# Token block sums in two column halves, and another product order in the first weight pair, in an encoder block in float32

## The chip, the cores and the metric

The kernel runs on one core of one Trainium2 chip. The metric is the device time of one execution in microseconds; the median of three runs of the kernel before is 762.26 us (760.61 to 762.30). The engines are called by name: TensorE (PE in the rows) multiplies, VectorE (DVE) adds and subtracts, ScalarE (ACT) copies, rounds and applies functions, GpSimd (POOL) does small odd jobs and issues some DMAs, and SyncE (SP) issues the loads.

## What is computed

A transformer encoder block on 512 tokens of 1024 channels: two attention branches merged by gates, then a feed-forward stage. Only the last matters here.

```python
x = x + rmsnorm(merged @ w_out[l], post_mix_w[l])
h = rmsnorm(x, pre_ffn_w[l])
f = (jax.nn.silu(h @ w_gate[l]) * (h @ w_up[l])) @ w_down[l]
x = x + rmsnorm(f, post_ffn_w[l])
```

`w_gate` and `w_up` are 1024 x 2816. Everything is float32.

## The kernel before

**Precision.** TensorE takes operands rounded to float32r. So each operand is split into a high part (a rounded copy, made by ScalarE) and a low part (the rest, made by a subtraction on VectorE), and each product is three matmuls: high x high, high x low, low x high (`mm3`, L205 to L208, or L1016 to L1018).

**The tokens.** After the attention stage the loop at L918 takes four token tiles of 128. For each it multiplies by `w_out` and norms twice: `scaled` (L892) squares and scales the product, `post` (L903) adds it to x, sums the squares (`add_square`, L888), lets GpSimd make the reciprocal root (`rms_r`, L307), and scales the result to `h2` (L913). `to_Q` (L856) transposes `h2` on TensorE (L864), and writes the high part (L866), the low part (L867) and a float32 copy (L868, `HR`). The tokens are held as four blocks B11, B12, B21, B22: the first index is the half of the 1024 channels, the second the half of the 512 tokens. Token tiles 0 and 1 make the columns of B11 and B21, tiles 2 and 3 those of B12 and B22, 128 columns each.

**The feed-forward stage.** The first 256 columns of `w_gate` and of `w_up` (`UF`, four weight units) are multiplied in the plain way, first with the first half of the tokens and then with the second (loop at L976). Tile 3 is transposed in the middle of the last unit of the first half (L985), and the token sums follow (`t_sums`, L872). The other columns come as 20 pairs of weight tiles, gate and up in turn (loop at L1005). Each pair is a 2 x 2 block product made in seven products of blocks instead of eight, by the Strassen-Winograd scheme: the weight blocks A11 to A22 are combined to S1 to S4, the token blocks to T1 to T4. A product is 12 matmuls of 128 x 256 columns (four steps of 128 channels, three matmuls each), so a pair is 84. The token sums are made once for all pairs:

```python
for nm, a, b in (("T1", b12, b11), ("T2", b22, "T1"), ("T3", b22, b12), ("T4", b21, "T2")):
    t[nm] = U(F32, [128, 4, 256], "Tr")
    nc.vector.tensor_sub(t[nm], a, t[b] if isinstance(b, str) else b)
```

with a high part `Th` (L880) and a low part `Tl` (L881) of each.

**The weights of a pair** are prepared in six steps (`pair_steps`, L63), one behind each product of the pair ahead; for the first pair they are spread over the second half of the loop at L976 (L992, L993). Step `s0` splits A11 and A12 together: ScalarE makes the high part (L70) and a negated copy of it (L72), and GpSimd issues a DMA that adds the raw weights to the negated copy, which gives the low part (L73). `s1` adds S2 and S1 on VectorE (L94, L95), `s2` splits them (L70, and L75 on VectorE), `s3` and `s4` do the same for S3 and S4 (L105, L106), and `s5` splits A22, by DMA again. The parts of S3 and S4 are kept in the place of the second half's upper token block `Q[0, 1]`, which the pairs don't read.

**Order.** Up to the end of the value projections the order is written by hand. From there on a scheduler orders each engine's queue by its own estimate of times, keeping the dependencies; so the written order of the stages here is only its input. Each engine works through its queue in order. Eight PSUM banks (`psB`) go round among the transposes, the first feed-forward columns and the pairs.

Of the kernel before, what the change touches and what calls it, by code (L numbers as in the profile page):

```python
# [8 lines left out]
F32 = mybir.dt.float32  # L9
F32R = mybir.dt.float32r  # L10
AF = mybir.ActivationFunctionType
# [4 lines left out]
D = 1024  # L16
# [16 lines left out]
def dram(ap, offset, pattern):  # L33
    return bass.AP(tensor=ap.tensor, offset=ap.offset + offset, ap=pattern)
# [136 lines left out]
def block_kernel(ctx: ExitStack, tc: tile.TileContext, x, pre_mix_w, w_in,  # L171
# [3 lines left out]
    nc = tc.nc  # L175
# [22 lines left out]
    def U(dt, shape, name, pool=None):  # L198
        return (pool or up).tile(shape, dt, tag="u", name=name)
# [5 lines left out]
    def mm3(bank, sh, sl, mh, ml, first, last):  # L205
        nc.tensor.matmul(bank, sh, mh, start=first, stop=False)  # L206
        nc.tensor.matmul(bank, sh, ml, start=False, stop=False)  # L207
        nc.tensor.matmul(bank, sl, mh, start=False, stop=last)  # L208
# [15 lines left out]
    for nm, c0 in (("vb", 2560), ("va", 1024)):  # L224
        for j in range(4):
            n = w_in.shape[1]
            src = dram(w_in, c0 + 2 * j * 128 * n,
                       [[n, 128], [128 * n, 2], [1, 512]])
# [131 lines left out]
    v = {}  # L360
# [441 lines left out]
    psB = pstk.enter_context(tc.tile_pool(name="psB", bufs=6, space=PSUM))  # L802
# [11 lines left out]
    for m in range(8):  # L814
        bank = pmm.tile([128, 512], F32, tag="mm", name="mm")
# [4 lines left out]
        hi, lo = W.get(UG["a", m])  # L820
# [4 lines left out]
        hi, lo = W.get(UBR["a", m // 2])  # L825
        cs = slice(128 * (m % 2), 128 * (m % 2) + 128)
# [4 lines left out]
        t = U(F32R, [128, 2, 512], "mg")  # L831
# [6 lines left out]
    psB = ctx.enter_context(tc.tile_pool(name="psC", bufs=8, space=PSUM))  # L838
# [6 lines left out]
    for b in range(NB):  # L845
        t = U(F32, [128, D], "x2")
# [7 lines left out]
    HR = {}  # L854

    def to_Q(h, b):  # L856
        n, cs = b // 2, slice(128 * (b % 2), 128 * (b % 2) + 128)
        for g in range(2):
            if (g, n) not in HR:
                HR[g, n] = U(F32, [128, 4, 256], "HR")  # L860
            tb = psB.tile([128, 4, 128], F32, tag="b", name="tb")
            for k in range(4):
                kk = 4 * g + k
                nc.tensor.transpose(tb[:, k], h[:, 128 * kk:128 * kk + 128], ident)  # L864
            hi, lo, raw = Q[g, n][:, 0, :, cs], Q[g, n][:, 1, :, cs], HR[g, n][:, :, cs]
            nc.scalar.activation(hi, tb, AF.Copy)  # L866
            nc.vector.tensor_sub(lo, tb, hi.bitcast(F32))  # L867
            nc.scalar.activation(raw, tb, AF.Copy)  # L868

    TQ = {}  # L870

    def t_sums():  # L872

        b11, b12, b21, b22 = HR[0, 0], HR[0, 1], HR[1, 0], HR[1, 1]
        t = {}
        for nm, a, b in (("T1", b12, b11), ("T2", b22, "T1"), ("T3", b22, b12), ("T4", b21, "T2")):
            t[nm] = U(F32, [128, 4, 256], "Tr")
            nc.vector.tensor_sub(t[nm], a, t[b] if isinstance(b, str) else b)
            hi, lo = U(F32R, [128, 4, 256], "Th"), U(F32R, [128, 4, 256], "Tl")
            nc.scalar.activation(hi, t[nm], AF.Copy)  # L880
            nc.vector.tensor_sub(lo, t[nm], hi.bitcast(F32))  # L881
            TQ[nm] = hi, lo
        for nm, q in (("B11", Q[0, 0]), ("B21", Q[1, 0]), ("B22", Q[1, 1])):
            TQ[nm] = q[:, 0], q[:, 1]

# [32 lines left out]
    for b in range(NB):  # L918
# [6 lines left out]
        for n, k0, k1 in parts:  # L925
            if b and n == 1 and k0 == 4:
                to_Q(h2[b - 1], b - 1)
            for k in range(k0, k1):
                hi, lo = W.get(UO[k])
# [13 lines left out]
    F = []  # L943

    def ff_out(G, Uu):

        f = U(F32, [128, 2, 512], "f", up2 if len(F) < 11 else up)
        nc.scalar.activation(f, G, AF.Sigmoid)
        nc.vector.tensor_mul(f, f, G)
        nc.vector.tensor_mul(f, f, Uu)  # L950
        F.append(f)
# [13 lines left out]
    def steps_of(n):  # L965
        if n >= len(pairs):
            return []
        return W.pair_steps(pairs[n], lambda: U(F32, [128, 1024], "S"))
# [7 lines left out]
    for half in range(2):  # L976
        cs = slice(256 * half, 256 * half + 256)
        for m in range(2):
            for nm in ("g", "u"):
                last = half == 0 and m == 1 and nm == "u"  # L980
                bank = bb[nm, m][:, cs]
                hi, lo = W.get(UF[nm, m])
                for k in range(KD):
                    if last and k == 4:
                        to_Q(h2[3], 3)  # L985
                        t_sums()
                    q = Q[k // 4, half]
                    mm3(bank, hi[:, k], lo[:, k], q[:, 0, k % 4], q[:, 1, k % 4],
                        k == 0, k == KD - 1)
                if half == 1:  # L990
                    W.drop(UF[nm, m])
                    first = first or steps_of(0)  # L992
                    first.pop(0)()  # L993
    for fn in first:
        fn()
    G, Uu = U(F32, [128, 2, 512], "G"), U(F32, [128, 2, 512], "G")
    for m in range(2):
# [1 line left out]
        nc.vector.tensor_copy(Uu[:, m], bb["u", m])  # L999
    ff_out(G, Uu)  # L1000

    ORDER = (("A11", "B11", "A"), ("S2", "T2", "B"), ("S1", "T1", "C"), ("S3", "T3", "D"),
             ("S4", "B22", "C"), ("A12", "B21", "A"), ("A22", "T4", "D"))
    gu = {}
    for n, unit in enumerate(pairs):  # L1005
        nxt = steps_of(n + 1)
        parts = W.parts.pop(unit)
        bank = {c: psB.tile([128, 512], F32, tag="b", name="b")[:, :256] for c in "ABCD"}
        G = U(F32, [128, 2, 512], "G")
        pv = U(F32, [128, 3, 256], "pv")  # L1010
        for i, (sn, tn, c) in enumerate(ORDER):
            (sh, sl), (th, tl) = parts[sn], TQ[tn]
            for k in range(4):
                fst, lst = i < 4 and k == 0, k == 3
                kw = {"skip_group_check": True} if i >= 4 else {}
                nc.tensor.matmul(bank[c], sh[:, k], th[:, k], start=fst, stop=False, **kw)  # L1016
                nc.tensor.matmul(bank[c], sh[:, k], tl[:, k], start=False, stop=False, **kw)  # L1017
                nc.tensor.matmul(bank[c], sl[:, k], th[:, k], start=False, stop=lst, **kw)  # L1018
            B = bank[c]
            if i == 0:  # L1020
                nc.scalar.activation(pv[:, 0], B, AF.Copy)
            elif i == 1:
                nc.vector.tensor_add(pv[:, 1], pv[:, 0], B)
            elif i == 2:
                nc.vector.tensor_add(pv[:, 2], pv[:, 1], B)
            elif i == 3:
                nc.vector.tensor_add(G[:, 1, 256:], pv[:, 2], B)
            elif i == 4:
                nc.vector.tensor_add(G[:, 0, 256:], pv[:, 1], B)
            elif i == 5:  # L1030
                nc.scalar.activation(G[:, 0, :256], B, AF.Copy)
            else:
                nc.vector.tensor_add(G[:, 1, :256], pv[:, 1], B)
            if nxt:
                nxt.pop(0)()
        gu[n % 2] = G
        if n % 2:
            ff_out(gu[0], gu[1])
# [42 lines left out]
    for b in range(NB):  # L1081
        f_split()
        t = U(F32, [128, D], "x2")
        nc.sync.dma_start(t, x2d[b])
        x2.append(t)
    for b in range(NB):
# [6 lines left out]
        for n in range(2):  # L1093
            c = slice(512 * n, 512 * n + 512)
# [71 lines left out]
```

## Time and profile before

| | kernel before |
|---|---|
| median of 3 runs | 762.26 us (760.61 to 762.30) |
| the profiled execution | 761.96 us |
| its span in the profile | 760.0 us |
| TensorE busy | 738.8 us (97%) |
| VectorE busy | 481.5 us (63%) |
| ScalarE busy | 373.8 us (49%) |
| GpSimd busy | 85.1 us (11%) |
| mean of all DMA traffic | 134 GB/s |

Busy shares are over the whole span; the change concerns a stretch of some 30 us around 425 us, where the pairs begin. Times in the rows are microseconds from the start of the span. In a row of the timeline the first number is the start, the second the duration, and the bracket at its end tells how long the engine had been idle before and what it then waited for. `x2` is two instructions in one row.

### The profile page before, as it was taken

How to read it: one execution, taken by the hardware profiler on the slowest of the kernel's cores; microseconds unless marked ns; L12 is line 12 of the kernel's file. 1: busy time of each engine (PE TensorE's matmuls, PEld its weight loads, DVE VectorE, ACT ScalarE, POOL GpSimd, SP SyncE). 2: the span in 40 equal slices, each digit the busy share in tenths (PEclk: the TensorE clock that was granted, in tenths of full speed). 3: DMA queues.
4: the chain of work that ended last, by engine and by line, in shares of the span. 5: the costliest groups of instructions: out<-in, count | busy, mean ns of one | idle time of the engine just before them, and what ended most of it. 6: DMA issues, size and time to landing. Idle time of an engine off the chain costs nothing.

```text
span 760.0 us, 11245 instructions
## 1 busy us (share of the span) xinstructions
PE 738.8 (97%) x4360; PEld 650.6 (86%) x4360; DVE 481.5 (63%) x827; ACT 373.8 (49%) x604; POOL 85.1 (11%) x130
## 2 busy tenths in 40 slices
PE   7999999999999999999999799999999999999996
PEld 5887888877888888887889799999999998888884
DVE  5625688888776633564456787778877789232333
ACT  4414565665666732452224566666666667222211
POOL 2001011122330000000110111111111110000000
PEclk9999999999999999999999899999999999999998
DMA  9537646333311122464514487778788774453112
GB/s 257 171 98 201 159 124 160 98 97 97 97 56 57 56 83 84 131 201 131 147 55 139 97 164 180 182 177 196 174 193 194 183 197 149 138 167 109 58 41 70
DMA packets 102724, 102.01 MB, mean 134 GB/s; under 512 B 3552, under 2 KB 85488, under 8 KB 102672
## 3 DMA queue, kind: packets, MB, share of 16 engines
q1 hardware_dynamic: 96224, 83.34, 38.0%
q0 software_dynamic: 6448, 17.97, 12.2%
q8 instruction: 34, 0.56, 0.3%
q14 instruction: 18, 0.15, 0.1%
HBM read 75.08 MB, written 4.19 MB: 104 GB/s over the span
## 4 chain that ended last, share of the span: by engine, by line
PE 85%; DVE 6%; ACT 4%; DMA 2%; issue 1%; SPq 0%; POOL 0%; DVEq 0%; POOLq 0%; ACTq 0%
PE b L1016 9%; PE b L1018 9%; PE b L206 9%; PE b L1017 9%; PE b L208 9%; PE b L207 9%; PE mm L206 7%; PE mm L208 7%; PE mm L207 7%; PE mm L375 5%; DMA raw<-in_w_in_dram 2%; PE s L669 1%; DVE pl L620 1%; ACT p L586 1%; PE t L708 1%
## 5 line engine op out<-in xcount | busy, mean ns | idle before, releaser
L146 DVE TENSOR_TENSOR w<-raw,w 128x1024 fp32r<-128x1024 f32 x67 | 82.1, 1226 | 85.4 <-ACT w L140 84.9
L140 ACT ACTIVATE w<-raw 128x1024 fp32r<-128x1024 f32 x67 | 70.4, 1053 | 64.3 <-PE b L208 52.6
L206 PE MATMUL mm<-hT,w 128*128 128x512 f32 x256 | 101.3, 396 | 0.2 <-DVE v L387 0.2
L208 PE MATMUL mm<-hT,w 128*128 128x512 f32 x256 | 100.6, 393 | 0.0
L207 PE MATMUL mm<-hT,w 128*128 128x512 f32 x256 | 100.1, 391 | 0.0
L1016 PE MATMUL b<-Th,w 128*128 128x256 f32 x240 | 68.8, 287 | 4.5 <-ACT w L70 4.5
L1018 PE MATMUL b<-Th,w 128*128 128x256 f32 x240 | 68.8, 288 | 0.0
L1017 PE MATMUL b<-Tl,w 128*128 128x256 f32 x240 | 68.6, 286 | 0.0
L208 PEld LDWEIGHTS mm<-hT,w 128*128 128x128 f32 x256 | 48.1, 188 | 10.7
L206 PEld LDWEIGHTS mm<-hT,w 128*128 128x128 f32 x256 | 48.1, 188 | 10.3 <-DVE v L387 0.6
L207 PEld LDWEIGHTS mm<-hT,w 128*128 128x128 f32 x256 | 48.1, 188 | 9.9
L206 PE MATMUL b<-w,fh 128*128 128x512 f32 x144 | 56.1, 390 | 0.0
L208 PE MATMUL b<-w,fl 128*128 128x512 f32 x144 | 56.1, 390 | 0.0
L207 PE MATMUL b<-w,fh 128*128 128x512 f32 x144 | 56.0, 389 | 0.0
L73 POOL DMA_DIRECT2D w<-raw x40 | 34.5, 862 | 177.5 <-ACT w L72 110.4
L1016 PEld LDWEIGHTS b<-Th,w 128*128 128x128 f32 x240 | 46.7, 195 | 4.7 <-ACT w L70 4.7
L1018 PEld LDWEIGHTS b<-Th,w 128*128 128x128 f32 x240 | 46.9, 196 | 0.0
L1017 PEld LDWEIGHTS b<-Tl,w 128*128 128x128 f32 x240 | 46.7, 194 | 0.0
L1016 PE MATMUL b<-Q,w 128*128 128x256 f32 x160 | 44.5, 278 | 0.0
L1017 PE MATMUL b<-Q,w 128*128 128x256 f32 x160 | 44.4, 278 | 0.0
L1018 PE MATMUL b<-Q,w 128*128 128x256 f32 x160 | 44.4, 278 | 0.0
L896 ACT ACTIVATE junk<-b 128x512 f32<-128x512 f32 x16 | 9.6, 597 | 62.5 <-PE b L208 57.6
(221 smaller groups left out, 1884.0 us busy)
## 6 DMA issues: line engine op xcount, KB each, us to landing
raw<-in_w_in_dram SPq DMA_DIRECT2D x40, 512.0 KB, 4.0
raw<-in_w_gate_dram SPq DMA_DIRECT2D x22, 512.0 KB, 4.2
raw<-in_w_up_dram SPq DMA_DIRECT2D x22, 512.0 KB, 5.0
raw<-in_w_down_dram SPq DMA_DIRECT2D x22, 512.0 KB, 3.3
w<-raw POOLq DMA_DIRECT2D x20, 512.0 KB, 6.4
K<-K SPq DMA_DIRECT2D x24, 256.0 KB, 3.2
w<-raw POOLq DMA_DIRECT2D x20, 256.0 KB, 7.7
x<-in_x_dram SPq DMA_DIRECT2D x8, 512.0 KB, 9.5
```

The lines of the kernel that those rows point to most:

```text
L73: nc.gpsimd.dma_start(lo, src, accum_op=ALU.add)
L140: self.nc.scalar.activation(hi, raw, AF.Copy)
L146: (engine or self.nc.vector).tensor_sub(lo, raw, hi.bitcast(F32))
L206: nc.tensor.matmul(bank, sh, mh, start=first, stop=False)
L207: nc.tensor.matmul(bank, sh, ml, start=False, stop=False)
L208: nc.tensor.matmul(bank, sl, mh, start=False, stop=last)
L375: nc.tensor.matmul(bank, hT[k // 4][:, k % 4, pa, 128 * b:128 * b + 128], W.get(UV[nm, k // 2])[pw][:, k % 2], start=n == 0, stop=n == len ...
L586: nc.scalar.activation(pw, pw, AF.Exp, bias=sm[:, hd:hd + 1], scale=-1.0, accum_out=sm[:, 2 + hd:3 + hd])
L896: nc.scalar.activation(junk, bs, AF.Square, scale=1.0 / 32.0, accum_out=ss[:, n:n + 1])
L1016: nc.tensor.matmul(bank[c], sh[:, k], th[:, k], start=fst, stop=False, **kw)
L1017: nc.tensor.matmul(bank[c], sh[:, k], tl[:, k], start=False, stop=False, **kw)
L1018: nc.tensor.matmul(bank[c], sl[:, k], th[:, k], start=False, stop=lst, **kw)
```

## The change

`t_sums` gets an argument, the column half. Half 0 takes the first 128 of the 256 columns of each block (token tiles 0 and 2) and is called right behind the first weight unit of the first half; half 1 takes the other 128 columns (tiles 1 and 3) where the whole sum stood. The first pair gets an order of its own, ORDER0: A11 B11, then A12 B21 and S4 B22, which read no token sums, and then the four products with T. A12 B21 and S4 B22 get PSUM banks of their own (F and E), and C11 and C12 are put together from other banks. The first pair's loop issues the second pair's six steps behind products two to seven. All other pairs keep their order.

```diff
-    TQ = {}
-
-    def t_sums():
-
-        b11, b12, b21, b22 = HR[0, 0], HR[0, 1], HR[1, 0], HR[1, 1]
-        t = {}
-        for nm, a, b in (("T1", b12, b11), ("T2", b22, "T1"), ("T3", b22, b12), ("T4", b21, "T2")):
-            t[nm] = U(F32, [128, 4, 256], "Tr")
-            nc.vector.tensor_sub(t[nm], a, t[b] if isinstance(b, str) else b)
-            hi, lo = U(F32R, [128, 4, 256], "Th"), U(F32R, [128, 4, 256], "Tl")
-            nc.scalar.activation(hi, t[nm], AF.Copy)
-            nc.vector.tensor_sub(lo, t[nm], hi.bitcast(F32))
-            TQ[nm] = hi, lo
+    TQ, TR = {}, {}
+
+    def t_sums(half):
+
+
+        cs = slice(128 * half, 128 * half + 128)
+        src = {"B11": HR[0, 0], "B12": HR[0, 1], "B21": HR[1, 0], "B22": HR[1, 1]}
+        for nm, a, b in (("T1", "B12", "B11"), ("T2", "B22", "T1"),
+                         ("T3", "B22", "B12"), ("T4", "B21", "T2")):
+            if half == 0:
+                TR[nm] = U(F32, [128, 4, 256], "Tr")
+                TQ[nm] = U(F32R, [128, 4, 256], "Th"), U(F32R, [128, 4, 256], "Tl")
+            src[nm] = TR[nm]
+            t, (hi, lo) = TR[nm][:, :, cs], (x[:, :, cs] for x in TQ[nm])
+            nc.vector.tensor_sub(t, src[a][:, :, cs], src[b][:, :, cs])
+            nc.scalar.activation(hi, t, AF.Copy)
+            nc.vector.tensor_sub(lo, t, hi.bitcast(F32))
...
-                        t_sums()
+                        t_sums(1)
...
+                if half == 0 and m == 0 and nm == "g":
+                    t_sums(0)
...
-    ORDER = (("A11", "B11", "A"), ("S2", "T2", "B"), ("S1", "T1", "C"), ("S3", "T3", "D"),
-             ("S4", "B22", "C"), ("A12", "B21", "A"), ("A22", "T4", "D"))
+    ORDER = (("A11", "B11", "A", "p"), ("S2", "T2", "B", "v"), ("S1", "T1", "C", "v5"),
+             ("S3", "T3", "D", "c22"), ("S4", "B22", "C", "c12"), ("A12", "B21", "A", "c11"),
+             ("A22", "T4", "D", "c21"))
+
+    ORDER0 = (("A11", "B11", "A", "p"), ("A12", "B21", "F", "p11"), ("S4", "B22", "E", ""),
+              ("S2", "T2", "B", "v"), ("S1", "T1", "C", "v5 p12"), ("S3", "T3", "D", "c22"),
+              ("A22", "T4", "D", "c21"))
...
-        bank = {c: psB.tile([128, 512], F32, tag="b", name="b")[:, :256] for c in "ABCD"}
+        bank = {}
...
-        for i, (sn, tn, c) in enumerate(ORDER):
+        for i, (sn, tn, c, ev) in enumerate(ORDER if n else ORDER0):
+            opens = c not in bank
+            if opens:
+                bank[c] = psB.tile([128, 512], F32, tag="b", name="b")[:, :256]
...
+                elif what == "p12":
+                    nc.vector.tensor_add(G[:, 0, 256:], pv[:, 2], bank["E"])
...
+                elif what == "p11":
+                    nc.vector.tensor_add(G[:, 0, :256], pv[:, 0], bank["F"])
...
-            if nxt:
+            if nxt and (n or i):
                 nxt.pop(0)()
```

What the scheduler makes of it stands in the queues. VectorE between the squares of the last token tile and the S additions of the first pair (`Tr` a token sum, `Tl` its low part, `Q` the low part of the last tile's tokens, `S` a sum of weight blocks), before:

```order
L888 ISA h_3524,ss_3523<-x_3184,ss_3523 128x512
L888 ISA ss_3523 128x1
L913 SCALAR_TENSOR_TENSOR h_3524<-x_3184,ss_3523,pfw 128x512 x2
L867 TENSOR_TENSOR Q<-tb,Q 128x4x128 x2
L878 TENSOR_TENSOR Tr<-HR 128x1024
L881 TENSOR_TENSOR Tl<-Tr,Th 128x1024
...
L878 TENSOR_TENSOR Tr<-HR,Tr 128x1024
L881 TENSOR_TENSOR Tl<-Tr,Th 128x1024
L94 TENSOR_TENSOR S<-raw 128x512
L105 TENSOR_TENSOR S<-raw 128x512
L95 TENSOR_TENSOR S<-S,raw 128x512
```

and now:

```order
L892 ISA ss_3523 128x1
L884 TENSOR_TENSOR Tr<-HR 128x4x128
L917 SCALAR_TENSOR_TENSOR h_3524<-x_3184,ss_3523,pfw 128x512 x2
L886 TENSOR_TENSOR Tl<-Tr,Th 128x4x128
...
L884 TENSOR_TENSOR Tr<-HR 128x4x128
L867 TENSOR_TENSOR Q<-tb,Q 128x4x128 x2
L886 TENSOR_TENSOR Tl<-Tr,Th 128x4x128
...
L94 TENSOR_TENSOR S<-raw 128x512
L886 TENSOR_TENSOR Tl<-Tr,Th 128x4x128 x2
L95 TENSOR_TENSOR S<-S,raw 128x512
L105 TENSOR_TENSOR S<-raw 128x512
L106 TENSOR_TENSOR S<-raw,S 128x512
```

One half sum now stands ahead of the scaling of the last tile, four half operations between that and the tile's low part, nine behind it up to L94, and two between L94 and L95.

ScalarE from the first token sum's high part (`Th`) to the negated copy of the second pair's A11 and A12 (`w<-raw` is a high part of raw weights, L72 the negated copy, `w<-S` and `Q<-S` the high parts of the weight sums, `G<-b` a PSUM copy), before:

```order
L880 ACTIVATE Th<-Tr 128x1024 x3
L70 ACTIVATE w_3799<-raw 128x512
L998 ACTIVATE G<-b 128x512
L72 ACTIVATE w_3799<-w_3799 128x512
L70 ACTIVATE w<-S 128x1024
L998 ACTIVATE G<-b 128x512
L70 ACTIVATE Q<-S 128x1024
L948 ACTIVATE f<-G 128x1024
L1021 ACTIVATE pv<-b 128x256
L70 ACTIVATE w<-raw 128x1024
L72 ACTIVATE w<-w 128x1024
```

and now:

```order
L885 ACTIVATE Th<-Tr 128x4x128 x2
L70 ACTIVATE w_3811<-raw 128x512
L70 ACTIVATE w<-S 128x1024
L72 ACTIVATE w_3811<-w_3811 128x512
L1004 ACTIVATE G<-b 128x512
L70 ACTIVATE Q<-S 128x1024
L1004 ACTIVATE G<-b 128x512
L70 ACTIVATE w<-raw 128x1024
L952 ACTIVATE f<-G 128x1024
L1037 ACTIVATE pv<-b 128x256
L72 ACTIVATE w<-w 128x1024
```

The high part of the second pair's A11 and A12 (`w<-raw`, 128x1024) has moved ahead of the sigmoid (`f<-G`) and of the first pair's `pv` copy; its negated copy stays behind both.

TensorE at the start of the second pair (`b_3953` is that pair's A11 B11, `b_3971` its S2 T2, `b_3914` the first pair's A22 T4), now:

```order
L1031 MATMUL b_3953<-Q_3186,w_3859 128x256 [waits PE_49,Activation_49]
L1033 MATMUL b_3953<-Q_3186,w_3859 128x256
L1034 MATMUL b_3953<-Q_3186,w_3859 128x256 [waits DMASW1_49]
...
L1031 MATMUL b_3971<-Th_3583,w_3893 128x256 [waits Activation_49]
L1031 MATMUL b_3914<-Th_3595,w22_3811 128x256 [waits DVE_49]
L1033 MATMUL b_3914<-Tl_3596,w22_3811 128x256
L1034 MATMUL b_3914<-Th_3595,w22_3811 128x256 [waits DMASW0_49]
```

Before, A22 T4 of the first pair stood ahead of all of the second pair; now the second pair's A11 B11 and one matmul more come first. Ahead of this piece the products of the first pair stand in the written order of ORDER0, 12 matmuls each. SyncE's and GpSimd's queues have the same order as before.

## Rows read from the trace of the kernel before

**Rows 1.** Waits of TensorE from 420 to 600: total us, times, longest us.

```profile
PE b L1016 <- ACT w L70: 4.5, 1, 4.5
PE b L1016 <- ACT Q L70: 0.7, 1, 0.7
```

**Rows 2.** Timeline of TensorE around the first pair.

```profile
413.81 0.28 PE L207 MATMUL b<-Q,w 128*128 128x256 f32 x1
...
425.00 0.28 PE L1016 MATMUL b<-Q,w 128*128 128x256 f32 x1
...
431.08 0.39 PE L1016 MATMUL b<-Th,w 128*128 128x256 f32 x1 [4.50 <-ACT w L70]
...
432.51 0.58 PE L1016 MATMUL b<-Th,Q 128*128 128x256 f32 x1 [0.69 <-ACT Q L70]
...
443.34 0.28 PE L1016 MATMUL b<-Q,w 128*128 128x256 f32 x1
```

**Rows 3.** Stretches: length, busy us of each engine, granted clock, DMA share, GB/s.

```profile
433.00:434.00 1.00, 1.00 (x7) 1.00 (x7) 1.00 (x2) 1.00 (x3) 0.00 (x0) 0.50 1.04 309
446.00:466.00 20.00, 19.98 (x169) 19.77 (x168) 16.34 (x25) 13.34 (x18) 3.43 (x4) 1.00 0.90 183
```

**Rows 4.** Timeline of VectorE from the last token tile to the S additions.

```profile
407.94 0.08 DVE L888 DVE_READ_ACCUMULATOR2_ANT ss<- 128x1 f32 x1
408.77 1.41 DVE L913 SCALAR_TENSOR_TENSOR h<-x,ss,pfw 128x512 f32<-128x512 f32 x2 [0.74 <-POOL ss L307]
412.67 1.29 DVE L867 TENSOR_TENSOR Q<-tb,Q 128x512 fp32r<-128x512 f32 x2 [2.49 <-ACT Q L866]
...
416.38 1.22 DVE L881 TENSOR_TENSOR Tl<-Tr,Th 128x1024 fp32r<-128x1024 f32 x1 [1.13 <-ACT Th L880]
...
427.99 0.68 DVE L94 TENSOR_TENSOR S<-raw 128x512 f32<-128x512 f32 x1
428.59 0.68 DVE L105 TENSOR_TENSOR S<-raw 128x512 f32<-128x512 f32 x1
```

**Rows 5.** Timeline of ScalarE in the same stretch.

```profile
417.82 1.06 ACT L72 ACTIVATE w<-w 128x1024 fp32r<-128x1024 f32 x1
...
430.93 0.58 ACT L998 ACTIVATE G<-b 128x512 f32<-128x512 f32 x1
431.41 1.05 ACT L70 ACTIVATE Q<-S 128x1024 fp32r<-128x1024 f32 x1
432.35 1.05 ACT L948 ACTIVATE f<-G 128x1024 f32<-128x1024 f32 x1
433.30 0.37 ACT L1021 ACTIVATE pv<-b 128x256 f32<-128x256 f32 x1
433.56 1.06 ACT L70 ACTIVATE w<-raw 128x1024 fp32r<-128x1024 f32 x1
```

**Rows 6.** Timeline of GpSimd: the DMAs for the first two pairs' low parts.

```profile
419.18 0.94 POOL L73 DMA_DIRECT2D w<-raw  x1 [10.45 <-ACT w L72]
...
436.00 0.85 POOL L73 DMA_DIRECT2D w<-raw  x1 [6.50 <-ACT w L72]
```

**Rows 7.** Us to landing of the DMAs issued at 436.00, 450.28 and 460.23.

```profile
w<-raw POOLq DMA_DIRECT2D x1, 512.0 KB, 4.6
...
w<-raw POOLq DMA_DIRECT2D x1, 512.0 KB, 5.7
...
w<-raw POOLq DMA_DIRECT2D x1, 512.0 KB, 6.5
```

**Rows 8.** Two waits of TensorE at the start, and stretches behind them.

```profile
8.40 1.91 PE L323 MATMUL tb<-ident,h 128*128 128x128 f32 x8 [2.25 <-DVE h L356]
15.03 1.20 PE L375 MATMUL mm<-whi,hT 128*128 128x512 f32 x4 [1.33 <-ACT whi L140]
8.50:12.00 3.50, 3.50 (x12) 2.58 (x13) 2.83 (x5) 2.14 (x3) 0.00 (x0) 0.51 1.04 279
12.00:20.00 8.00, 6.45 (x31) 4.55 (x30) 6.40 (x7) 4.35 (x6) 3.69 (x2) 1.00 1.04 298
```

More of the change, by code (lines that the diff above doesn't have):

```diff
@@ L1007, in block_kernel @@
         parts = W.parts.pop(unit)
-        bank = {c: psB.tile([128, 512], F32, tag="b", name="b")[:, :256] for c in "ABCD"}
+        bank = {}
         G = U(F32, [128, 2, 512], "G")
         pv = U(F32, [128, 3, 256], "pv")
-        for i, (sn, tn, c) in enumerate(ORDER):
+        for i, (sn, tn, c, ev) in enumerate(ORDER if n else ORDER0):
+            opens = c not in bank
+            if opens:
+                bank[c] = psB.tile([128, 512], F32, tag="b", name="b")[:, :256]
             (sh, sl), (th, tl) = parts[sn], TQ[tn]
+            kw = {} if opens else {"skip_group_check": True}
@@ L1013, in block_kernel @@
             for k in range(4):
-                fst, lst = i < 4 and k == 0, k == 3
-                kw = {"skip_group_check": True} if i >= 4 else {}
-                nc.tensor.matmul(bank[c], sh[:, k], th[:, k], start=fst, stop=False, **kw)
+                nc.tensor.matmul(bank[c], sh[:, k], th[:, k], start=opens and k == 0,
+                                 stop=False, **kw)
                 nc.tensor.matmul(bank[c], sh[:, k], tl[:, k], start=False, stop=False, **kw)
-                nc.tensor.matmul(bank[c], sl[:, k], th[:, k], start=False, stop=lst, **kw)
@@ L1019, in block_kernel @@
[L1019 to L1033, printed above, removed]
@@ L1034, in block_kernel @@
-            if nxt:
+                nc.tensor.matmul(bank[c], sl[:, k], th[:, k], start=False, stop=k == 3, **kw)
+            for what in ev.split():
+                if what == "p":
+                    nc.scalar.activation(pv[:, 0], bank["A"], AF.Copy)
+                elif what == "v":
+                    nc.vector.tensor_add(pv[:, 1], pv[:, 0], bank["B"])
+                elif what == "v5":
+                    nc.vector.tensor_add(pv[:, 2], pv[:, 1], bank["C"])
+                elif what == "c22":
+                    nc.vector.tensor_add(G[:, 1, 256:], pv[:, 2], bank["D"])
+                elif what == "c12":
+                    nc.vector.tensor_add(G[:, 0, 256:], pv[:, 1], bank["C"])
+                elif what == "p12":
+                    nc.vector.tensor_add(G[:, 0, 256:], pv[:, 2], bank["E"])
+                elif what == "c11":
+                    nc.scalar.activation(G[:, 0, :256], bank["A"], AF.Copy)
+                elif what == "p11":
+                    nc.vector.tensor_add(G[:, 0, :256], pv[:, 0], bank["F"])
+                else:
+                    nc.vector.tensor_add(G[:, 1, :256], pv[:, 1], bank["D"])
```

## The prediction

> **What bounds the kernel now.** I read the waits of TensorE first, then its timeline around the longest of them, then what VectorE, ScalarE and GpSimd did in that stretch. TensorE hardly ever stops, so only its own gaps and its clock can be won. From 420 us to 600 us the waits name two gaps, one directly after the other: 4.5 us for a ScalarE copy on L70 and 0.7 us for another [rows 1]. The timeline puts both into the first weight pair [rows 2]: its first product (A11 B11, 12 matmuls) starts at 425.00, the next one only at 431.08, and one more hole opens before 432.51. The second pair starts at 443.34. So the first pair took 443.34 - 425.00 = 18.34 us. In the undisturbed stretch from 446 to 466 the same kind of matmul comes every 20.00/169 = 0.118 us [rows 3], so 84 matmuls are worth 9.94 us. **The first pair loses 18.34 - 9.94 = 8.40 us**: 4.50 + 0.69 = 5.19 us of waiting, and 3.21 us because the granted clock is 0.50 after the wait (the 1.2 GHz level; 7 matmuls in a microsecond where full clock does 8 to 9) [rows 3].
>
> Why does TensorE wait? Its second product needs a sum of the pair's own weight blocks (S), and on VectorE the S additions stand behind the token sums: the last token tile reaches VectorE at 412.67, then eight token-sum instructions of 128x1024 run, each low part waiting about 1.1 us for ScalarE, and the first S addition starts at 427.99 [rows 4]. The S parts are split on ScalarE after that, the last at 431.41 [rows 5].
>
> **What the change does to VectorE's queue.** The token sums become 16 instructions of half size. A 128x512 addition takes 0.68 us and the next one follows after 0.60 us (427.99 to 428.59) [rows 4]; so the 16 cost about 9.6 us of VectorE. Now part by part.
>
> (1) The first half sum stands between the square sums of the last token tile (last one at 407.94, 0.08 us) and its scaling (408.77), where VectorE waits 0.74 us for GpSimd [rows 4]. It ends at 408.02 + 0.68 = 408.70, before 408.77: nothing. If it did not fit, the scaled tile still has cover: it is done at 408.77 + 1.41 = 410.18.
>
> (2) Four more half operations come ahead of the two subtractions that make the low part of that tile (412.67 today). 410.10 + 4 x 0.60 = 412.50, plus one handoff through ScalarE (sum done 411.38, its high part about 0.6 us, as the copy of 512 columns at 430.93 [rows 5], so the low part starts at 412.06 and not 411.31): the subtractions start at 413.26. That is 0.59 us later. Their first half takes 1.29/2 = 0.65 us, so the low part is there at 413.91 and not 413.32, and TensorE reads it at 413.81 [rows 2]. **Loss: about 0.15 us** (0 to 0.3).
>
> (3) Then 15 half operations to the last S addition: nine of token sums, L94, two more, then L95, L105 and L106, without a gap if ScalarE's high parts keep up (by the same durations each is ready 0.3 us or more ahead). The two subtractions end by 414.48, so L95 ends at 414.48 + 13 x 0.60 + 0.08 = 422.36 and L106 at 423.56; today L95 only starts after 428.59.
>
> (4) ScalarE then makes the high part of S2 and S1 at 422.40, two small copies, and the high part of S3 and S4 at 424.35 to 425.40. VectorE needs 1.22 us for the low part, as at 416.38 [rows 4]: 426.65. TensorE, in the new order, takes A11 B11 and A12 B21 first and comes to S4 B22 at 425.15 + 24 x 0.118 = 427.98. **Slack 1.3 us, so the 4.50 and the 0.69 us go, and with them the 3.21 us of half clock.** The other products of the pair read parts that are older still. Six PSUM banks are opened in the first pair instead of four; the four taken over from the first feed-forward columns are emptied by L1004 and L1005 between 424 and 427.3, each before its use (428 to 432.2). VectorE has one more addition of 0.4 us, ScalarE one copy less: both beside TensorE's work.
>
> (5) The low part of A11 and A12 of the first pair comes by a GpSimd DMA, started at 419.18 after the negated copy of 417.82 [rows 5, 6]. In the new ScalarE queue four half-size high parts stand ahead; the third sum's comes at 417.00, the copy to be negated at 417.5, the negated copy 1.1 us later, at 418.6 instead of 417.82, and the DMA 0.8 us later than today. TensorE needs it in the third matmul, at 425.24 today without waiting, so it was there by then and is there by 426.0 at the latest: a wait of 0 to 0.65 us. The transfer started almost six microseconds ahead, so I take 0.
>
> **What is late next.** The second pair's low part travels the same way, and its cover is gone. Today its DMA starts at 436.00 [rows 6] and TensorE wants it only at 443.34 + 0.24. Changed, ScalarE comes to its negated copy after the high part of S3 and S4 (424.35): that copy and four others (a PSUM copy, the second pair's high part, the sigmoid, a small PSUM copy) cost 0.95 + 0.48 + 0.95 + 0.95 + 0.27 us, so it starts at 427.95 and ends at 429.01. (These are times from one start to the next, 430.93 to 431.41 to 432.35 to 433.30 to 433.56; a copy by itself lasts 1.06 [rows 5].) The DMA follows 0.3 us later, as at 419.18 after 418.88: 429.3. TensorE is there much earlier than today: in the new order the second pair's A11 B11 stands ahead of the last product of the first pair, 72 matmuls after its start, 425.15 + 72 x 0.118 = 433.67, and the third matmul needs the low part at 433.9. TensorE works in order, so the product behind it can't fill the hole. From issue to landing such a 512 KB transfer took 4.6 us (the one at 436.00), 5.7 us and 6.5 us [rows 7]; it lands at 433.9, 435.0 or 435.8, a **wait of 0, 1.1 or 1.9 us**. I take 1.1: 4.6 us was a transfer with none behind it in its queue, whereas here a second GpSimd DMA follows 1.2 us later, as in the case of 5.7 us. Behind this nothing is short: the third pair's low part would be issued at about 436.6 and is wanted at 446.
>
> A wait of this size leaves the clock alone by the rows: at the start of the kernel TensorE waited 2.25 us before 8.40 and ran the next 3.5 us at a granted clock of 0.51, but 1.33 us before 15.03 within a stretch at 1.00 [rows 8].
>
> **The sum.** 8.40 - 0.15 - 0 - 1.1 = 7.15 us. The profiled execution took 761.96 us (span 760.0 and 1.96 around it); it becomes 754.8. The median of the runs is 762.26, 0.3 above the profiled one, so I forecast **755.1 us**.
>
> The Trainium skill, DMA: Bandwidth & Descriptors, section Anatomy of one DMA - SWDGE (gpsimd) path, gives such a transfer as 2.0 us plus its bytes over 436 GB/s. As an estimate from that page, 512 KB would take 3.2 us, there would be no wait in the second pair, and the sum would be 8.25. The rows have 4.6 to 6.5 us and are what I go by.
>
> **Rivals.**
> (a) The second pair's low part comes in time. For it: 4.6 us is the row of this very transfer. Against it: the following DMA. It gives 8.40 - 0.15 = 8.25, that is 754.0 us. The page's 3.2 us leads to the same result.
> (b) The wait at the second pair is longer and the clock falls again. For it: 6.5 us has a row, and ScalarE has no idle time ahead of the copy; against it: GpSimd's queue is free. With 1.9 us or more, and 3.4 us at half clock behind it as after the 2.25 us wait (1.7 us lost), 8.40 - 0.15 - 1.9 - 1.7 = 4.65: 757.6 us; with the 0.65 of step 5 as well, 758.3.
> (c) It doesn't do what it says: the scaled tile or ScalarE's extra handoffs hold VectorE, the S parts come some 4 us later than in step 4, and TensorE's hole only moves behind the second product. Then a wait of about 3 us and the half clock stay: 8.40 - 3 - 3.2 = 2.2 or less, 760 to 762 us.
> (d) **Slower.** A half instruction, whose 512 elements lie in four pieces of 128, costs what a whole one does. Sixteen at 1.14 us instead of 0.60 put VectorE 8 us behind step 4; S4's low part would come at 434.7 against 428.2 wanted. That wait of 6.5 us with the 3.2 us of half clock, and about 1.6 us that the second half of the first feed-forward columns would wait for its low parts, make 11.3 us against today's 8.40: 765 us. It decides from about 1.0 us a piece on, where the gain is used up. Against it: the two subtractions at 412.67 write just such pieces and take 1.29 us together [rows 4].
>
> **How the numbers follow.** Forecast 0.50, (a) 0.22, (b) 0.18, (c) 0.06, (d) 0.04. The range reaches from rival (a) at the foot of the runs' scatter (754.0, less 1.2) to (b) with everything late (758.3): 752.8 to 758.4, which holds the forecast, (a) and most of (b). A measurement tells 0.3%, 2.3 us, from no change. Forecast, (a) and (b) lie beyond it, and a little of (c): faster 0.91; the rest of (c) is no change, 0.05; (d) slower, 0.04.
>
> **What would show it.** In the changed profile TensorE's list of waits has no 4.5 us for L70; S4 B22 runs straight on; the second pair starts about 8.5 us after the first; the granted clock has no 0.50 near 432; a wait for a w DMA of about 1 us stands in the third matmul of the second pair (L1034); the half sums last 0.68 us; GpSimd's second DMA of a 512 KB low part starts near 429.3. Wrong would be a wait of over 2 us anywhere between 425 and 440, or one that is new in a later pair.

## The result: 756.9 us

The changed kernel takes 756.88 us in the median of 4 runs (756.36 to 758.18), the kernel before 761.60 (760.61 to 762.30) beside it: a ratio of 0.9948, 95% interval 0.9935 to 0.9960. It is faster by half a per cent, with an interval that leaves out no change; the time is inside the range and 1.8 us above the forecast of 755.1. The profiled execution took 757.20 us with a span of 755.0, against 761.96 and 760.0: 5.0 us less span, where 7.15 were forecast.

The waits of TensorE from 405 to 600 us in the changed kernel (line, what it waited for: total us, times, longest us):

```profile
PE b L1034 <- DMA w<-raw: 2.5, 1, 2.5
PE b L207 <- DVE Q L867: 0.4, 1, 0.4
```

Both gaps of [rows 1] are gone, and two others stand there. The timeline of TensorE in the same kernel shows where:

```profile
413.71 0.28 PE L206 MATMUL b<-Q,w 128*128 128x256 f32 x1
414.36 0.39 PE L207 MATMUL b<-Q,w 128*128 128x256 f32 x1 [0.37 <-DVE Q L867]
414.58 0.28 PE L208 MATMUL b<-Q,w 128*128 128x256 f32 x1
...
425.65 0.28 PE L1031 MATMUL b<-Q,w 128*128 128x256 f32 x1
...
428.48 0.28 PE L1031 MATMUL b<-Q 128*128 128x256 f32 x1
...
434.33 0.28 PE L1033 MATMUL b<-Q,w 128*128 128x256 f32 x1
437.10 0.39 PE L1034 MATMUL b<-Q,w 128*128 128x256 f32 x1 [2.49 <-DMA w<-raw]
```

The first pair starts at 425.65 and runs without a stop through S4 B22 (428.48), where the kernel before stood still for 4.50 us [rows 2]. The new waits are in the last token tile's place (414.36) and in the third matmul of the second pair (437.10). The stretches ahead of, in and behind the second of them, by length, busy us of each engine, granted clock, DMA share and GB/s, are at full clock, against the 0.50 of [rows 3]:

```profile
431.00:432.00 1.00, 1.00 (x11) 1.00 (x10) 1.00 (x2) 0.00 (x0) 0.77 (x1) 1.00 0.51 110
434.00:436.00 2.00, 0.61 (x6) 0.40 (x4) 2.00 (x5) 2.00 (x3) 0.00 (x0) 1.00 1.03 206
436.00:438.00 2.00, 0.90 (x7) 0.90 (x8) 1.59 (x2) 0.68 (x1) 0.85 (x1) 1.00 0.79 142
```

What the two waits cost is read from one start to the next. With a pitch of 0.118 us the matmul at 414.36 was due at 413.83, and the one behind it came 0.10 late again: 0.53 + 0.10 = 0.63 (the rows are rounded; 0.64 is used below). The one at 437.10 was due at 434.45: 2.65 + 0.10 = 2.75. The account of the stage is then 8.40 - 0.64 - 2.75 = 5.01 us, and the span fell by 5.0.

**One measure for all kernels.** Executions differ by up to 2.5 us in how late the stage begins (407.06 us in e2, 409.60 in e10; the longest wait at the kernel's start is 1.8 us in the one and 3.5 in the other). So I also give the length of the stage in the one profiled execution of each kernel: from the start of the last square sum of the last token tile on VectorE to the first matmul of the down projection. In the kernel before it is 632.50 - 407.27 = 225.23 us, in the changed one 627.55 - 407.28 = 220.27.

| kernel | median us | ratio to before (95%) | stage, us | regained, us |
|---|---|---|---|---|
| the change | 756.88 | 0.9948 (0.9935 to 0.9960) | 220.27 | 4.96 |
| e1 split only | 755.15 | 0.9923 (0.9907 to 0.9938) | 218.11 | 7.12 |
| e2 order only | 760.25 | 0.9995 (0.9986 to 1.0004) | 224.02 | 1.21 |
| e3 low part by VectorE | 755.25 | 0.9924 (0.9908 to 0.9940) | 217.69 | 7.54 |
| e4 load held back | 756.62 | 0.9947 (0.9926 to 0.9968) | 219.48 | 5.75 |
| e5 sum behind the power | 757.46, one run | | 220.77 | 4.46 |
| e6 split, low by VectorE | 755.00 | 0.9909 (0.9894 to 0.9925) | 217.52 | 7.71 |
| e8 sums around the tile | 754.26 | 0.9897 (0.9879 to 0.9914) | 217.04 | 8.19 |
| e9 one delay | 756.42, one run | | 219.15 | 6.08 |
| e10 three delays | 761.94, one run | | 222.73 | 2.50 |

### The profile page after: what moved, and what is told of

Its sections match the earlier page's. It is cut to its first block, busy times and chain, and to the rows that moved or that the text cites. A ratio compares the mean times of both kernels' runs of the same rounds, so it can differ in the third digit from the quotient of the medians.

```text
span 755.0 us, 11252 instructions
## 1 busy us (share of the span) xinstructions
PE 736.7 (98%) x4360; PEld 648.1 (86%) x4360; DVE 482.9 (64%) x836; ACT 373.9 (50%) x607; POOL 85.7 (11%) x130
## 5 line engine op out<-in xcount | busy, mean ns | idle before, releaser
L1034 PE MATMUL b<-Th,w 128*128 128x256 f32 x240 | 67.9, 283 | 0.0
L1031 PE MATMUL b<-Th,w 128*128 128x256 f32 x240 | 67.7, 283 | 0.0
L1034 PEld LDWEIGHTS b<-Th,w 128*128 128x128 f32 x240 | 45.9, 191 | 0.0
L1031 PEld LDWEIGHTS b<-Th,w 128*128 128x128 f32 x240 | 45.8, 191 | 0.0
L307 POOL TENSOR_TENSOR ss<-ss,mhalf 128x1 f32<-128x1 f32 x16 | 9.1, 568 | 279.7 <-DVE ss L902 254.5
```

The source lines that it names most:

```text
L307: nc.gpsimd.tensor_tensor(r, ss, mhalf[:, :1], op=ALU.pow)
L1031: nc.tensor.matmul(bank[c], sh[:, k], th[:, k], start=opens and k == 0, stop=False, **kw)
```

## The experiments

### Which part of the change does it: e1 and e2

e1 keeps the halved sums and gives the first pair the old order; e2 keeps the whole sums of the kernel before and takes only the new order.

```diff
-        for i, (sn, tn, c, ev) in enumerate(ORDER if n else ORDER0):
+        for i, (sn, tn, c, ev) in enumerate(ORDER):
...
-            if nxt and (n or i):
+            if nxt:
```

> The token sums in two halves as in the changed kernel, but every pair, the first too, in the old product order. Theory A (splitting the sums is what brings the first pair's weight sums forward; the new order is not needed for it): TensorE reaches S2 T2 near 427.1 and S3 T3 near 429.9, their parts are there at about 425.2 and 427.1, so no wait in the first pair. The first pair's last product now stands ahead of the second pair's first, so the second pair's low part is wanted 1.4 us later, and the wait for it falls from 2.5 to about 1.2 us: about 755.8 us, 0.992 to 0.994 of before. Theory B (the new order carries a good part of the gain): a wait of 2 us or more behind the first product, 759 us or more.

> The new product order in the first pair, the token sums whole and in their old place. Theory A: the weight sums start near 428 as before, S4's parts come near 432 to 434, TensorE stands at S4 B22 from 427.8 on, 4 to 6 us, and its clock falls to 0.50 behind it; 760 to 762 us, 0.997 to 1.001 of before (at best the 1.4 us of one product more in front of the wait are won). Theory B: half of the gain or more, 759 us or less.

The waits of e1 from 405 to 600 us, and then TensorE's timeline of e2 at its wait, with a stretch behind it:

```profile
PE b L1034 <- DMA w<-raw: 0.6, 1, 0.6
PE b L207 <- DVE Q L867: 0.4, 1, 0.4
```

```profile
432.31 0.58 PE L1025 MATMUL b<-Q 128*128 128x256 f32 x1 [4.53 <-ACT Q L70]
```

```profile
432.00:434.00 2.00, 1.70 (x7) 1.56 (x8) 2.00 (x3) 2.00 (x4) 0.00 (x0) 0.50 0.88 251
```

The split alone closes the big hole: 7.12 us of the stage come back, 2.2 more than with the new order beside it. The order alone only moves the hole: the wait is 4.53 us instead of 4.50, the clock falls as before, 1.21 us of the stage come back since one wait is left instead of two, and the time is the same within its interval. What the new order costs is at the second pair. In e1 the second pair's A11 B11 stands behind the last product of the first, so its low part is wanted at 435.97 and not 434.45; the transfer lands nearly as late as in the change (436.7 and 437.1), but the wait is 0.61 instead of 2.49. The two waits show this, not the times alone: the intervals of e1 and the change just touch.

### What the second pair waits for: e3, e4, e6

e3 is the change, with the low part of the second pair's A11 and A12 made by a VectorE subtraction instead of the GpSimd DMA. e6 is e1 with the same edit.

```diff
-            high_low(hi, lo, r0, True)
+            high_low(hi, lo, r0, j != self.vec_low)
...
+    W.vec_low = UP["u", 1]
```

> The changed kernel, with the low part of A11 and A12 of the second pair made by a VectorE subtraction instead of the negated copy and the GpSimd DMA. Theory C (the 2.5 us wait in the second pair is that transfer alone): the wait goes, nothing takes its place, 754.4 us, 0.990 to 0.992 of before. Theory D (with the transfer gone the second pair's weight sums on VectorE, 1.1 us later, are late next): a new wait of 1 us or more in the second pair, 756 us or more.

> Halved sums with the old order for every pair, and the second pair's first low part made by VectorE instead of a GpSimd DMA. Theory A and C together (the split gives the gain, and what is left at the second pair is the DMA alone): the 0.6 us wait that the split alone leaves at the second pair goes, nothing takes its place, the span is 752.4 and the time 754.5 (754.0 to 755.2). Rival: VectorE is then too late with the first pair's evictions or the next sums, a wait of 0.3 to 1 us on VectorE appears in the first or second pair, and the time is 755 to 756, no better than the split alone (755.15).

In both, one wait is left from 400 to 600 us (e3 here; e6 has the same row):

```profile
PE b L208 <- DVE Q L868: 0.4, 1, 0.4
```

So nothing is late behind the DMA: VectorE had room for one more 1.22 us subtraction, and the stage is 217.69 and 217.52 us. With the 0.64 of the first wait the account closes to 0.2 us again: 7.54 + 0.64 = 8.18 and 7.71 + 0.64 = 8.35. In time e6 can't be told from e1 (755.00 and 755.15); in the stage it is 0.6 us shorter, as expected.

Why the DMA took 7.3 us is the next question. The prediction put a longer landing down to the second GpSimd DMA behind it. But a 512 KB load of SyncE was issued 0.2 us after it. The queues of GpSimd and SyncE in the changed kernel, and the time to landing of both:

```profile
429.73 0.86 POOL L73 DMA_DIRECT2D w<-raw  x1 [4.15 <-ACT w L72]
430.91 0.85 POOL L73 DMA_DIRECT2D w<-raw  x1 [0.33 <-ACT w L72]
```

```profile
429.92 7.63 SPq L128 DMA_DIRECT2D raw<-in_w_up_dram  x2
```

```profile
w<-raw POOLq DMA_DIRECT2D x1, 512.0 KB, 7.3
raw<-in_w_up_dram SPq DMA_DIRECT2D x1, 512.0 KB, 6.9
```

e4 is the change with this load held back until a sum of the first pair is there, by a one-column copy of that sum into the load's tile, and with one load less ahead up to there; the GpSimd DMA behind is left.

```diff
+            if self.gate is not None:
+                self.nc.vector.tensor_copy(raw[:, 0:1], self.gate)
...
+    W.raw_bufs = 4
...
+            if n == 0 and i == 4:
+                W.gate = pv[:, 2, 0:1]
+                W.raw_bufs = 5
+                W.load_to(UP["u", 2] + 1)
```

> The changed kernel, but the 512 KB load that was issued at 429.92, 0.2 us behind the second pair's low-part DMA, is held back until the first pair's third sum is done (a one-column copy on VectorE that the load waits for, near 434 to 436). Theory E (the low-part DMA took 7.3 us because the load moved beside it): it lands in 4.6 to 5.7 us, the wait of 2.5 us falls to 0 to 0.9 us, 754.5 to 755.5 us. Theory F (the second GpSimd DMA behind it, or the DMA itself, sets the 7.3 us): landing 7 us or more, the wait stays at 2 us or more, 757 us.

The next two loads and the copy in e4:

```profile
434.69 1.46 SPq L132 DMA_DIRECT2D raw<-in_w_up_dram  x2
```

```profile
435.61 0.14 DVE L129 COPY raw<-pv 128x1 f32<-128x1 f32 x1
```

The held-back load is the second of the two: it goes out at 435.78, behind the copy. The one at 434.69 is the load that in the change follows the low part's DMA at 437.2. Neither is issued before that DMA has landed. Time to landing of the low part's DMA in e4, issued at 429.94, then TensorE's wait and ScalarE's timeline:

```profile
w<-raw POOLq DMA_DIRECT2D x1, 512.0 KB, 4.6
```

```profile
PE b L1036 <- DVE pv L1046: 1.6, 1, 1.6
```

```profile
442.52 1.06 ACT L71 ACTIVATE w<-raw 128x1024 fp32r<-128x1024 f32 x1 [2.18 <-DMA raw<-in_w_up_dram]
```

With the load out of its way the DMA lands in 4.6 us, with the 256 KB GpSimd DMA behind it as in the change (issued at 431.12). So it was the load, and not the DMA that follows. The wait at the second pair is gone, yet the time is the change's: 1.6 us come back as a wait at 453.79, for a sum on VectorE. ScalarE had waited 2.18 us for the held-back load, and the sum's place in VectorE's queue is behind the work that this load feeds. Counted from the start of the stage, the sum comes 1.56 us later than in e3 (453.31 - 407.50 against 452.32 - 408.07). That one led to the other I read from the order of the rows; it was not tried by itself.

### The first wait: e5 and e8

In the change the half sum stands beside GpSimd's reciprocal root. VectorE and GpSimd in the changed kernel:

```profile
407.95 0.69 DVE L884 TENSOR_TENSOR Tr<-HR 128x512 f32<-128x512 f32 x1
409.09 1.42 DVE L917 SCALAR_TENSOR_TENSOR h<-x,ss,pfw 128x512 f32<-128x512 f32 x2 [0.45 <-POOL ss L307]
...
413.62 1.28 DVE L867 TENSOR_TENSOR Q<-tb,Q 128x512 fp32r<-128x512 f32 x2
...
423.24 0.69 DVE L106 TENSOR_TENSOR S<-raw,S 128x512 f32<-128x512 f32 x1
...
425.87 1.23 DVE L75 TENSOR_TENSOR Q<-S,Q 128x1024 fp32r<-128x1024 f32 x1
```

```profile
403.63 0.54 POOL L307 TENSOR_TENSOR ss<-ss,mhalf 128x1 f32<-128x1 f32 x1 [8.79 <-DVE ss L902]
...
408.19 0.87 POOL L307 TENSOR_TENSOR ss<-ss,mhalf 128x1 f32<-128x1 f32 x1 [1.70 <-DVE ss L892]
```

The half sum ends at 408.64, before 408.77, as forecast. But the same GpSimd power that takes 0.54 us at 403.63 takes 0.87 at 408.19, and the scaling starts 0.32 us later than in [rows 4]. e5 puts a one-column copy from the norm's result ahead of the first half sum, so that no half sum can run there:

```diff
+            if half == 0 and nm == "T1":
+                nc.vector.tensor_copy(TR[nm][:, 0, 0:1], root[0][:, 3:4])
```

> The change, with a one-element copy from the norm's result into T1's tile ahead of T1's first half, so that no half sum runs beside GpSimd's power; VectorE now does the whole scaling of the last token tile before the first half sum. Theory G (VectorE's half sum, both operands in SBUF, slows the power that runs beside it): the power goes from 0.87 back to 0.54 to 0.55 us and the scaling starts at 408.8 instead of 409.09. Rival H (the 0.87 us is chance or comes from elsewhere): it stays at 0.8 or more. For the whole: the half sums of T1 and T2 now come after the scaling and still stand ahead of the transposes' copy on ScalarE, so the low part of the last token tile should come about 1 us later than in the change and TensorE's first wait grow from 0.64 lost to some 1.5; with the second pair's wait unchanged the time is 757.5 to 758.5, no better than the change's 756.9.

GpSimd and VectorE in e5:

```profile
408.21 0.56 POOL L307 TENSOR_TENSOR ss<-ss,mhalf 128x1 f32<-128x1 f32 x1 [1.70 <-DVE ss L894]
```

```profile
408.80 1.42 DVE L920 SCALAR_TENSOR_TENSOR h<-x,ss,pfw 128x512 f32<-128x512 f32 x2 [0.75 <-POOL ss L307]
...
414.90 1.28 DVE L867 TENSOR_TENSOR Q<-tb,Q 128x512 fp32r<-128x512 f32 x2
```

The power is back at 0.56 us and the scaling at 408.80: theory G. As a kernel e5 is no gain, as expected: the first half sum and its way through ScalarE now come behind the scaling and still ahead of the low part, which starts 1.3 us later than in the change.

e8 is e6 with e5's copy, and of the half sums only T1's is left ahead of the last token tile; the first halves of T2 to T4 stand behind its low part. A one-column copy from that part holds T2 there, and with it T4, which reads T2; T3 comes behind in the order.

```diff
+            if half == 0 and nm == "T2":
+                nc.vector.tensor_copy(TR[nm][:, 0, 0:1], Q[1, 1][:, 1, 3, 255:256].bitcast(F32))
...
-                    t_sums(0)
+                    t_sums(0, ("T1",))
...
+                        t_sums(0, ("T2", "T3", "T4"))
                         t_sums(1)
```

> As the kernel before last in this list (halved sums, old order, second pair's first low part by VectorE), but of the half sums only T1's stand ahead of the last token tile's copies, behind the power; the first halves of T2 to T4 stand behind its low part. Theory I (step 2's loss is what stands ahead of the low part on VectorE and ScalarE): the low part starts at 412.7 as in the kernel before, the 0.4 us wait on it goes, and the part of 0.64 us that was lost there comes back; the sums end about 0.9 us later, inside the slack of the fourth product, so the time is 753.9 (753.4 to 754.6). Rival J (the sums' slack is less than that): the wait on the low part goes but a new one of 0.3 to 1 us stands in the first pair, on the sums' parts, and the time stays at 754.5 to 755.2.

VectorE in e8, whose stage begins 0.81 us later than in the kernel before, and the stretch of the whole stage:

```profile
413.49 1.29 DVE L868 TENSOR_TENSOR Q<-tb,Q 128x512 fp32r<-128x512 f32 x2 [0.31 <-ACT Q L867]
```

```profile
405.00:625.00 220.00, 219.89 (x1858) 219.61 (x1857) 180.36 (x277) 140.05 (x190) 34.76 (x41) 1.00 0.78 183
```

413.49 - 0.81 = 412.68: the low part starts where it did in the kernel before (412.67 [rows 4]). TensorE is busy for 219.89 of 220.00 us, no wait is listed from 400 to 600, and 8.19 of the 8.40 us are back. Theory I; the sums' slack was enough. **e8 is the best kernel of the study: 754.26 us, 0.9897 (0.9879 to 0.9914) of the kernel before, an interval clear of the change's.** Its interval overlaps those of e1, e3 and e6; it is the stage that sets it apart from them.

### The clock and the delay: e9 and e10

The kernel before lost its clock behind a wait of 4.50 us, the change kept it behind one of 2.49. To make the wait longer, e9 puts one GpSimd operation, and e10 three, in front of the second pair's low-part DMA.

```diff
+                if late:
+                    nc.gpsimd.tensor_scalar(self.junk(), lo[:, :256].bitcast(F32), 0.25, None,
+                                            op0=ALU.mult)
                 nc.gpsimd.dma_start(lo, src, accum_op=ALU.add)
```

> The change, with one more GpSimd operation of about 0.8 us in front of the second pair's low-part DMA, so that TensorE's wait there grows from 2.49 to about 3.3 us. It is for the clock alone, which fell in the kernel before after a wait of 4.50 us and did not in the change after 2.49. Theory K (the clock falls from somewhere between 2.5 and 3.3 us of wait on): the granted clock reads 0.50 behind the wait for some microseconds, as in the kernel before (6.8 us), the loss is 3.4 more than the longer wait alone, and the time 760.5 to 761.5. Rival L (it does not fall yet at 3.3): the clock reads 1.00 throughout and the time is 757.5 to 758, the change's plus the wait.

GpSimd's queue in e9, the DMA's time to landing, and TensorE's wait:

```profile
431.03 1.79 POOL L77 DMA_DIRECT2D w<-raw  x2 [0.30 <-POOL junk L75]
```

```profile
w<-raw POOLq DMA_DIRECT2D x1, 512.0 KB, 5.3
```

```profile
PE b L1039 <- DMA w<-raw: 1.4, 1, 1.4
```

This missed its aim: the DMA goes out 1.3 us later than in the change and lands 0.7 us earlier, and the wait is shorter. The clock question stayed open, but the collision shows from the other side: the load, issued 0.87 us ahead, now landed in 3.8 us instead of 6.9, and the DMA in 5.3 instead of 7.3. e10 tried again.

> The change, with three GpSimd operations in place of one in front of the second pair's low-part DMA. With one of them (0.86 us) that DMA was issued at 431.03 instead of 429.73, yet landed in 5.3 us instead of 7.3, and TensorE's wait became shorter, 1.41 instead of 2.49 us. With three the issue is near 433.3, when the load beside it (3.8 us in that run) is about over. Theory E (transfers that move at the same time take each other's share): it then lands in 4.5 to 5.3 us, near 438, and TensorE waits 3.3 to 4.2 us from 434.6 on. On the clock, after such a wait: theory K (it falls somewhere between 2.5 and 3.5 us, as after 4.50 in the kernel before): the granted clock reads 0.50 for some microseconds and the time is 760 to 762; rival L: it reads 1.00 throughout and the time is 757.8 to 758.8.

TensorE's wait in e10, the DMA's landing (issued at 435.72, the load lands at 436.0), the stretches behind, and two matmuls at half clock:

```profile
440.40 0.39 PE L1041 MATMUL b<-Q,w 128*128 128x256 f32 x1 [3.48 <-DMA w<-raw]
```

```profile
w<-raw POOLq DMA_DIRECT2D x1, 512.0 KB, 4.6
```

```profile
440.00:441.00 1.00, 0.60 (x5) 0.60 (x6) 0.36 (x1) 0.00 (x0) 0.59 (x1) 1.00 1.09 195
441.00:442.00 1.00, 1.00 (x10) 1.00 (x9) 0.00 (x0) 0.12 (x1) 0.00 (x0) 0.86 1.01 163
442.00:443.00 1.00, 1.00 (x7) 1.00 (x6) 0.00 (x0) 0.27 (x1) 0.00 (x0) 0.50 1.01 202
...
445.00:446.00 1.00, 1.00 (x10) 1.00 (x9) 0.68 (x2) 0.89 (x1) 0.00 (x0) 0.93 1.00 289
```

```profile
442.29 0.42 PE L1041 MATMUL b<-Th,w 128*128 128x256 f32 x1
442.50 0.41 PE L1038 MATMUL b<-Th,w 128*128 128x256 f32 x1
```

The DMA, with hardly anything beside it, takes 4.6 us, as in e4. The wait is 3.48 us, and the clock falls to 0.50 from about 441.7 to 445.1: theory K. At half clock a matmul follows after 0.213 us instead of 0.118, so the 3.4 us hold 16 matmuls that would take 1.9 us: they lose 1.5 us. With the 0.99 us by which the wait is longer than the change's that is 2.5; the stage is 2.46 us longer. The median is no measure here, since this execution's stage began 2.3 us later than the change's.

## Why the prediction was right and where it was wrong

**The hole's size, 8.40 us: right.** The accounts of the kernels without the hole close on it to about a quarter of a microsecond: the change 4.96 + 0.64 + 2.75 = 8.35, and e8, which has no wait left, regains 8.19. Its split was a little off. A wait costs about 0.26 us more than its idle time (2.75 for 2.49), so of the 3.21 us put down to the clock some 0.5 belong to the two waits, an estimate. And "7 matmuls in a microsecond where full clock does 8 to 9" compares two counts: a stretch counts every matmul that reaches into it, and a stretch of 1 us at full clock counts 11 (431 to 432 above).

**(1) The first half sum costs nothing: wrong by 0.32 us.** It ended in time, but it was costed by VectorE's time alone. It stretched the GpSimd operation for which VectorE waits there from 0.55 to 0.87 us (e5).

**(2) The low part of the last token tile, 0.15 us: mis-sized, 0.64.** VectorE began it at 413.62 and not 413.26; 0.32 of the 0.36 is step 1's. So TensorE lost 0.15 + 0.36, and about 0.1 because a matmul behind a wait is followed 0.22 us later and not 0.118, which the step left out.

**(3), (4) The S parts: right.** The last S addition ended at 423.93 (423.56 worked out), the low part of S4 at 427.10 (426.65). S4 B22 wanted it at 428.48: a slack of 1.4 us against 1.3. But the slack was worked out for the new order alone. It was there in the old order too (e1), and this step did not ask what the order added. It added nothing in the first pair and took 1.9 us of wait in the second.

**(5) The first pair's DMA, 0: right.** It went out at 420.32, 1.1 us later than before and not 0.8, and the first pair's third matmul still follows at 425.89 without a wait.

**What is late next: right in place, wrong in size; this is the term that made most of the miss.** The second pair's third matmul waits for the low part's DMA, as forecast, 2.49 us and 2.75 with what follows instead of 1.1. The prediction's own sign of being wrong, a wait of over 2 us between 425 and 440, came with it. The DMA went out at 429.73 (429.3 forecast) and was wanted at 434.45 (433.9), so the two moved together to 0.12 us. The landing was 7.3 us and not 5.7. The forecast chose among the three landings of [rows 7] by the DMA behind on the same queue; e4 shows that this was the wrong cause. Nor could it choose: the 5.7 and the 6.5 both had a GpSimd DMA 1.2 us behind (451.47 and 461.41). The right cause was in the trace of before: in SyncE's queue there, loads were issued at 458.92 and about 2 us later, around the one that took 6.5 us, and at 447.34 and about 451.1, around the one that took 5.7, but none between 431.98 and about 441, around the one that took 4.6. The change moved a load too (431.98 to 429.92, to 0.2 us behind the DMA): it is issued when the DMA for the first pair's A22 has landed, and that one went out at 424.71 instead of 428.63. The forecast did not follow SyncE's queue.

The Trainium skill, DMA: Bandwidth & Descriptors, section Anatomy of one DMA - SWDGE (gpsimd) path, gives 2.0 us plus the bytes over 436 GB/s, from which 3.2 us is an estimate for 512 KB; here it took 4.6 us alone, so the measurement decides. The same page of the Trainium skill, section Queues, rings and completion order, says that each DMA engine takes packets in turn from the queues that have work for it; e4, e10 and the change agree, with 4.6 us alone and 7.3 us beside a load.

**The clock: it stayed up, but not for the reason given.** The forecast was made for a wait of 1.1 us, and read from [rows 8] that 1.33 us leaves the clock alone and 2.25 us does not. The wait was 2.49 us, and the clock stayed at 1.00. Rival (b) had both a longer wait and the fall; only the first came. By the prediction's own reading the fall belonged to it, so that it did not come is luck. The price that (b) put on it, 1.7 us, is near the 1.5 us of e10, behind 3.48 us. With those 1.5 us the change would be at 758.4, an estimate, the very end of the range.

**The sum.** 7.15 - 0.49 (step 2) - 1.65 (second pair) = 5.01, the span's 5.0.

## To carry to other kernels

When a change moves work earlier, follow every queue that it moves, the loads' too, and look for transfers that will now run at the same time: a collision can cost more than an early issue gains, and e9's DMA, issued 1.3 us later, landed 0.7 us sooner. Of a change in two parts, ask of each what it does without the other; here the second part only brought the next deadline nearer. An instruction put into another engine's gap is free only if it leaves that engine's work alone.

## What the runs showed of the hardware

- GpSimd's power on 128x1 takes 0.54 to 0.56 us, and 0.87 beside a VectorE subtraction that reads two SBUF tiles (0.86 to 0.87 in e6 and e9 too). Beside the VectorE multiplication at 403.40, which reads one operand from PSUM, it takes 0.54. The Trainium skill, GPSIMD Engine Reference, section Key points, names this: GpSimd shares its interfaces to SBUF with VectorE, with contention for VectorE's instructions with two SBUF inputs. The trace agrees, with 0.32 us here.
- The adding DMA of 512 KB lands in 4.6 us alone (e4, e10), 5.3 with a load issued 0.87 us ahead of it (e9), 6.5 with one 0.10 us ahead (e5), and 6.9 and 7.3 with a load 0.28 and 0.19 us behind it (e1, the change).
- The clock stayed full behind waits of 1.41 and 2.49 us in this stretch and fell behind 3.48 and 4.50. At the kernel's start it read 0.51 behind one of 2.25 us [rows 8], where TensorE had worked for 4.64 us ahead of the wait; so the wait's length alone does not tell. Why these differ was not tried.
